# Adaptive-norm columns of the first layer: from GpSimd and VectorE products to TensorE and VectorE, with the opening reordered

## The chip, the cores and the metric

One core of a Trainium2 chip runs the whole program. The metric is device microseconds (us) of one execution. Its engines are TensorE (PE; its weight loads are PEld), VectorE (DVE), ScalarE (ACT), GpSimd (POOL) and SyncE (SP), which here issues most transfers. TensorE's clock is granted at one of two levels, 1.2 and 2.4 GHz; the profile gives the granted share of 2.4 GHz as PEclk.

## What is computed

Two layers over 512 tokens of width 1024. What matters here is how a layer begins:

```python
c_act = jax.nn.silu(c)                                   # (1, 1024)
mod = (c_act @ w_ada[l] + b_ada[l])[:, None, :]          # 6 x 1024
shift1, scale1, gate1, shift2, scale2, gate2 = jnp.split(mod, 6, axis=-1)
h = rms_norm(x, norm1_g[l]) * (1.0 + scale1) + shift1
z = h @ w_in[l]                                          # 14 tiles of 128 columns
```

From z come windowed attention, a short convolution and a multi-scale pooling, one output projection, then a second norm with shift2 and scale2 and an expert layer that takes most of the time.

## The kernel before

x is held transposed, 1024 channels as 8 blocks of 128 partitions by 512 tokens. So shift1 and scale1 are 8 columns each (block c, 128 partitions by 1). Every fp32 operand of a projection is split in two fp32r tiles, a high part rounded to fp32r and a low part, the rest; a product is then three: high by high, high by low, low by high (`mm`, L292 to L294). For h the parts are `hh` and `hl`, for a weight tile (128 output columns of `w_in`, 128x1024) `wh` and `wl`, made by a cast on ScalarE (`prep_hi`, L264) and a subtraction (`prep_lo`, L273, on the engine that is passed).

`setup` (from L108) loads c, makes an identity and three iotas on GpSimd, computes silu of c, and spreads it over all partitions into `cact` (128x1024): eight diagonal tiles on VectorE (L154), eight fp32 products with a tile of 1/1024 on TensorE (L155), two evictions with a factor of 1024 on ScalarE (L156).

`mixer` for the first layer opens so. SyncE's queue gets the four pieces of x (L391), then the first 7 of 16 column tiles of w_ada (each 128 output channels by 1024 inputs, 512 KB, shift and scale of block 0, of block 1, and so on) into buffers that are only needed later, and 4 weight tiles in between. A transfer whose buffer is not free stops what is behind it on the queue. The squares of x go two by two: ScalarE squares (L466), VectorE adds the two (L467), and TensorE sums over channels with fp32 products (`norm_sum`, L349) into `ms`. Each column tile is then multiplied by `cact` and summed along its row. For a scale column VectorE does both in one instruction (L219); for a shift column GpSimd multiplies (L217) and ScalarE sums in `fix` (L452). Then `ada_fix` adds the bias (L226) and, for the scale, multiplies by the norm's gain (L229), all on 128x1. `rsqrt` (from L326) turns `ms` into `rn` by Ln and Exp on ScalarE and a Newton step on VectorE, in halves of 256 tokens. GpSimd makes the low parts of the first three weight tiles before the projection begins.

`norm_apply` is a generator: per block, x times scale times `rn` on VectorE (L367), the shift added on ScalarE, giving `hh` (L368), and `hl` on VectorE (L361), one block behind. `chunk_multi` runs the first three output tiles of the projection together: for each block c it calls `step(c)` (the fix of block c + 2, the next `norm_apply` step, two more columns), then three tiles by three products. After block 5 it prepares one more weight tile in the spare buffer `ch`. The order of the program is the order of each engine; the framework adds the waits. After these 72 products, the other tiles of the projection follow one by one (`chunk`), with the other columns of w_ada worked in by `bg`.

Of the kernel before, what the change touches and what calls it, by code (L numbers as in the profile page):

```python
# [10 lines left out]
F32 = mybir.dt.float32  # L11
# [11 lines left out]
P = 128  # L23
# [58 lines left out]
class Build:  # L82
# [24 lines left out]
    def setup(self):  # L107
        nc, cp, A = self.nc, self.cp, self.A  # L108
        t = lambda shape, dt, nm: cp.tile(shape, dt, name=nm, tag=nm)
        self.x = t([P, NC, S], F32, "x")  # L110
        self.hh = t([P, NC, S], F32R, "hh")
        self.hl = t([P, NC, S], F32R, "hl")
        self.hc = [self.hh[:, c] for c in range(NC)]
        self.lc = [self.hl[:, c] for c in range(NC)]
        self.eps = t([P, 1], F32, "eps")
        nc.vector.memset(self.eps, EPS)
        cc = t([P, NC], F32, "cc")
        nc.sync.dma_start(cc, A["c"])
        self.ident = t([P, P], F32, "ident")
        make_identity(nc, self.ident)  # L120
        self.onesD = t([P, P], F32, "onesD")
        nc.vector.memset(self.onesD, 1.0 / D)
        self.iota = t([P, P], F16, "iota")
        nc.gpsimd.iota(self.iota, pattern=[[1, P]], base=0, channel_multiplier=0,
                       allow_small_or_imprecise_dtypes=True)
        self.iota4 = t([P, P, 4], F16, "iota4")
        nc.gpsimd.iota(self.iota4, pattern=[[1, P], [0, 4]], base=0, channel_multiplier=0,
                       allow_small_or_imprecise_dtypes=True)
        self.iotaA = t([P, TOPK, TOPK], F16, "iotaA")
        nc.gpsimd.iota(self.iotaA, pattern=[[1, TOPK], [0, TOPK]], base=0, channel_multiplier=0,  # L130
                       allow_small_or_imprecise_dtypes=True)
        self.rn = t([P, S], F32, "rn")
        self.modp = {}
        self.ready_parts = set()
        self.par = {}
        for l in range(self.depth):
            for nm in ("b_ada", "norm1", "norm2"):
                w = 48 if nm == "b_ada" else 8
                b = t([P, w], F32, f"{nm}{l}")
                nc.gpsimd.dma_start(b, A[nm][l])  # L140
                self.par[nm, l] = b
# [6 lines left out]
        self.cact = t([P, D], F32, "cact")  # L148
        dg = self.wp.tile([P, NC, P], F32, tag="wr", name="dg", bufs=WR)
        for half in range(2):  # L150
            b = self.bankA()
            for j in range(4):
                c = half * 4 + j
                nc.vector.tensor_scalar(dg[:, c], self.ident, e[:, c:c + 1], None, ALU.mult)  # L154
                nc.tensor.matmul(b[:, j * P:(j + 1) * P], self.onesD, dg[:, c], start=True, stop=True)  # L155
            nc.scalar.activation(self.cact[:, half * 512:(half + 1) * 512], b, AF.Copy, scale=float(D))  # L156

    def setup2(self, tp):
        nc, cp, A = self.nc, self.cp, self.A
# [49 lines left out]
        self.nc.sync.dma_start(w, self.A["w_ada"][l, part * NC + c])  # L209
        return w  # L210

    def ada_col(self, l, part, c, w=None, pool=False):
        nc = self.nc
        if w is None:
            w = self.ada_load(l, part, c)
        if pool:
            nc.gpsimd.tensor_tensor(w, w, self.cact, ALU.mult)  # L217
            return
        nc.vector.scalar_tensor_tensor(w, w, 1.0, self.cact, ALU.mult, ALU.mult,  # L219
                                       accum_out=self.modp[l, part][:, c:c + 1])  # L220

# [80 lines left out]
            self.prep_lo(eng)  # L302
        self.mm(ps, w, hh, hl, width, range(NC), 0, NC - 1)

    def chunk_multi(self, pss, hh, hl, step, eng=None, spare=None):
        n = len(pss)
        while len(self.half) + len(self.ready) < n:
            self.prep_hi()
        while len(self.ready) < n:
            self.prep_lo(eng)  # L310
        ws = [self.ready.pop(0) for _ in range(n)]
        for c in range(NC):
            step(c)
            for ps, w in zip(pss, ws):
                self.mm(ps, w, hh, hl, S, [c], 0, NC - 1)
            if c == (3 if n < 3 else 5):
                hi, lo = spare or (None, None)
                self.prep_hi(hi)
                self.prep_lo(eng, lo)


    def tables(self):
# [54 lines left out]
    def mixer(self, l, ada):  # L377
        nc, tc, A, x = self.nc, self.tc, self.A, self.x
        hh, hl, hc, lc = self.hh, self.hl, self.hc, self.lc
        with tc.tile_pool(name=f"mix{l}", bufs=1) as mp, \  # L380
# [45 lines left out]
            ap1 = self.norm_apply(tmp_, x, l, 1)  # L426
            spare = None
            if l == 0:

                flat = lambda a: a.rearrange("p a b -> p (a b)")  # L430
                prs = [flat(t([P, 4, 384], F32, "pr", bufs=3))[:, 0:D] for _ in range(3)]
                ch_, qk_ = flat(ch), flat(qk)
                slots = [qk_[:, 0:D], qk_[:, D:2 * D], *prs, flat(trig), cst[:, 0:D]]
                slot = lambda k: slots[k if k < 7 else (k - 7) % 6]
                spare = (ch_[:, 0:D], ch_[:, D:2 * D])
                loaded, used = [0], [0]

                def col_load():
                    k = loaded[0]
                    if k < 2 * NC:  # L440
                        loaded[0] += 1
                        self.ada_load(0, k % 2, k // 2, slot(k))

                def col_use():
                    k = used[0]
                    if k < 2 * NC:
                        used[0] += 1
                        self.ada_col(0, k % 2, k // 2, slot(k), k % 2 == 0)

                def fix(c):  # L450
                    w = slot(2 * c)
                    nc.scalar.activation(w, w, AF.Copy, accum_out=self.modp[0, 0][:, c:c + 1])  # L452
                    for part in range(2):
                        self.ada_fix(0, part, c, c + 1)
                    while loaded[0] < 2 * NC and loaded[0] - (7 if loaded[0] < 13 else 6) <= 2 * c + 1:
                        col_load()

                for k in range(7):
                    col_load()
                    if k in (1, 3, 5, 6):  # L460
                        self.prep_raw()
                ms = bankC()
                for c in range(0, NC, 2):
                    sq = [tmp_(), tmp_()]
                    for z in range(2):
                        nc.scalar.activation(sq[z], x[:, c + z], AF.Square)  # L466
                    nc.vector.tensor_tensor(sq[0], sq[0], sq[1], ALU.add)  # L467
                    if c == 0:
                        self.norm_eps(sq[0])
                    self.norm_sum(ms, sq[0], c == 0, c == NC - 2)  # L470
                self.tables()
                for k in range(4):
                    col_use()
                self.prep_hi()
                self.prep_lo(nc.gpsimd)
                for c in range(2):
                    fix(c)
                self.rsqrt(tmp_, ms, P, self.rn)
                for k in range(2):
                    self.prep_hi()  # L480
                    self.prep_lo(nc.gpsimd)
                for k in range(2):
                    col_use()
                next(ap1)
                for k in range(2):
                    col_use()

                def step(c):
                    nonlocal pre
                    if c + 2 < NC:  # L490
                        fix(c + 2)
                    next(ap1, None)
                    for k in range(2):
                        col_use()
                    if c == 5:
                        pre = self.setup2(mp)
                        next(pre)
                        pre = self.stepper(pre)
                        loads()
            else:  # L500
                for k in range(2):
                    self.prep_raw()
                loads()
                step = lambda c: next(ap1, None)
            bg = self.stepper(ada)

# [15 lines left out]
            n0 = 3 if l == 0 else 2  # L522
            pss = [self.bankA(), self.bankA()] + ([bankB()] if l == 0 else [])
            self.chunk_multi(pss, hc, lc, step, nc.gpsimd, spare)
            next(ap1, None)
            for i in range(n0):
                qk_raw(i, pss[i])
            self.prep_hi()
# [756 lines left out]
def layout(inp):  # L1285
# [19 lines left out]
    o["norm1"] = cvec(f("norm1_g"), NC)  # L1305
    o["norm2"] = cvec(f("norm2_g"), NC)
    o["w_ada"] = np.ascontiguousarray(f("w_ada").transpose(0, 2, 1).reshape(L, 48, P, D))
    o["b_ada"] = cvec(f("b_ada"), 48)
    o["w_in"] = chunks(f("w_in")[:, :, cols])
    o["q_norm_g"] = f("q_norm_g")  # L1310
# [33 lines left out]
```

## Time and profile before

| | |
|---|---|
| median of 3 runs | 2924.76 us (2924.71 to 2928.68) |
| profiled execution | 2922.05 us, span 2920.3 us |
| TensorE busy | 2840.1 us, 97% of the span |
| VectorE / ScalarE / GpSimd busy | 82% / 43% / 31% |
| DMA | 782.74 MB, mean 268 GB/s |

The share of busy time is a mean over stages with different limits. The opening is the first 67 us or so, a small part of the span, and has to be read by itself in the timeline and in busy times by stretch. A releaser in brackets is what ended an engine's idle time before an instruction.

### The profile page before, as it was taken

How to read it: one execution, taken by the hardware profiler on the slowest of the kernel's cores; microseconds unless marked ns; L12 is line 12 of the kernel's file. 1: busy time of each engine (PE TensorE's matmuls, PEld its weight loads, DVE VectorE, ACT ScalarE, POOL GpSimd, SP SyncE). 2: the span in 40 equal slices, each digit the busy share in tenths (PEclk: the TensorE clock that was granted, in tenths of full speed). 3: DMA queues.
4: the chain of work that ended last, by engine and by line, in shares of the span. 5: the costliest groups of instructions: out<-in, count | busy, mean ns of one | idle time of the engine just before them, and what ended most of it. 6: DMA issues, size and time to landing. Idle time of an engine off the chain costs nothing.

```text
span 2920.3 us, 41477 instructions
## 1 busy us (share of the span) xinstructions
PE 2840.1 (97%) x15196; PEld 2479.3 (85%) x15196; DVE 2399.2 (82%) x4616; ACT 1267.5 (43%) x1774; POOL 911.5 (31%) x783
## 2 busy tenths in 40 slices
PE   5999999999999999999999999999999999999999
PEld 3667899998888888888866678999988888888887
DVE  7977999858888888888868689999588888887887
ACT  4343357763333333333342444687433333333332
POOL 5415500003334334434324243000133333333332
PEclk8999999999999999999999999999999999999999
DMA  6534257789999999999943323576899999999996
GB/s 231 167 108 125 90 174 257 247 308 324 346 353 370 347 347 361 358 354 358 324 133 132 106 82 118 191 256 249 296 345 337 341 341 332 339 338 345 330 337 223
DMA packets 312972, 782.74 MB, mean 268 GB/s; under 512 B 26784, under 2 KB 154176, under 8 KB 309696
## 3 DMA queue, kind: packets, MB, share of 16 engines
q1 hardware_dynamic: 218992, 438.68, 44.3%
q0 software_dynamic: 73920, 268.53, 25.0%
q10 hardware_dynamic: 19856, 72.88, 6.8%
q8 instruction: 119, 1.95, 0.3%
q14 instruction: 85, 0.70, 0.1%
HBM read 705.02 MB, written 74.97 MB: 267 GB/s over the span
## 4 chain that ended last, share of the span: by engine, by line
PE 81%; DVE 16%; ACT 1%; issue 1%; POOL 0%; DMA 0%; DVEq 0%; ACTq 0%; POOLq 0%
PE pa L292 13%; PE pa L294 13%; PE pa L293 13%; PE pb L1058 6%; PE pb L1059 6%; PE pb L1062 6%; PE pb L1061 6%; PE pb L1057 6%; PE pb L1060 6%; PE pb L1004 1%; PE pb L1005 1%; DVE I L1187 1%; DVE s L1183 1%; DVE I L1181 1%; DVE mx L686 1%
## 5 line engine op out<-in xcount | busy, mean ns | idle before, releaser
L292 PE MATMUL pa<-hh,wh 128*128 128x384 f32 (+1 forms) x2568 | 904.7, 352 | 28.0 <-ACT hh L368 24.4
L293 PE MATMUL pa<-hl,wh 128*128 128x384 f32 (+1 forms) x2568 | 892.3, 347 | 10.9 <-DVE hl L361 10.3
L294 PE MATMUL pa<-hh,wl 128*128 128x384 f32 (+1 forms) x2568 | 892.7, 348 | 2.2 <-DVE wl L273 2.2
L1039 DVE TENSOR_TENSOR vl<-vr,vh 128x1024 fp32r<-128x1024 f32 x256 | 313.6, 1225 | 287.4 <-ACT vh L1038 286.4
L292 PEld LDWEIGHTS pa<-hh,wh 128*128 128x128 f32 x2568 | 484.4, 189 | 70.0 <-ACT hh L368 26.7
L293 PEld LDWEIGHTS pa<-hl,wh 128*128 128x128 f32 x2568 | 484.4, 189 | 40.2 <-DVE hl L361 14.4
L294 PEld LDWEIGHTS pa<-hh,wl 128*128 128x128 f32 x2568 | 483.8, 188 | 23.9 <-DVE wl L273 2.8
L1038 ACT CAST vh<-vr 128x1024 fp32r<-128x1024 f32 x256 | 269.5, 1053 | 507.4 <-PE pb L1062 236.2
L1075 POOL DMA_INDIRECT row<-in_peer_u_dram,eidx x256 | 306.9, 1199 | 550.8 <-DVE acc L1088 408.9
L1084 POOL DMA_INDIRECT row<-in_peer_v_dram,eidx x256 | 307.8, 1202 | 462.9 <-DVE row L1079 412.6
L273 DVE TENSOR_TENSOR wl<-wr,wh 128x1024 fp32r<-128x1024 f32 x264 | 324.0, 1228 | 67.7 <-ACT wh L264 33.7
L264 ACT CAST wh<-wr 128x1024 fp32r<-128x1024 f32 x331 | 349.0, 1056 | 44.2 <-DMA wr<-in_peer_uT_dram 21.5
L1088 DVE SCALAR_TENSOR_TENSOR acc<-row,gw,acc 128x1024 f32<-128x1024 f32 x256 | 327.6, 1280 | 0.1
L1079 DVE SCALAR_TENSOR_TENSOR row<-row,htok 128x1024 f32<-128x1024 f32 x256 | 311.8, 1219 | 0.0
L1058 PE MATMUL pb<-vh,whi 128*128 128x512 f32 x768 | 300.7, 392 | 0.0
L1059 PE MATMUL pb<-vl,whi 128*128 128x512 f32 x768 | 300.5, 391 | 0.0
L1062 PE MATMUL pb<-vh,wlo 128*128 128x512 f32 x768 | 300.0, 391 | 0.0
L1061 PE MATMUL pb<-vh,wlo 128*128 128x512 f32 x768 | 299.3, 390 | 0.0
L1057 PE MATMUL pb<-vh,whi 128*128 128x512 f32 x768 | 298.9, 389 | 0.0
L1060 PE MATMUL pb<-vl,whi 128*128 128x512 f32 x768 | 298.5, 389 | 0.0
L832 ACT ACTIVATE ga<-pa 128x384 f32<-128x384 f32 x256 | 125.8, 491 | 387.5 <-PE pa L294 382.8
L1007 ACT ACTIVATE stg<-pb 128x512 f32<-128x512 f32 x192 | 198.3, 1162 | 33.3 <-PE pb L1005 27.6
(302 smaller groups left out, 3751.7 us busy)
## 6 DMA issues: line engine op xcount, KB each, us to landing
wr<-in_peer_uT_dram SPq DMA_DIRECT2D x256, 512.0 KB
vr<-in_peer_v_dram SPq DMA_DIRECT2D x256, 512.0 KB
Gd<-stg ACTq DMA_DIRECT2D x24, 2048.0 KB
adaw<-in_w_ada_dram SPq DMA_DIRECT2D x80, 512.0 KB
gtFalse<-Gd SPq DMA_DIRECT2D x36, 768.0 KB
Sd<-ga ACTq DMA_DIRECT2D x112, 192.0 KB
gtTrue<-Gd SPq DMA_DIRECT2D x28, 768.0 KB
gs<-Sd SPq DMA_DIRECT2D x112, 192.0 KB
```

Of the source, the lines that this page charges most:

```text
L264: self.nc.scalar.copy(hi, raw)
L273: (eng or self.nc.vector).tensor_tensor(lo, raw, hi.bitcast(F32), ALU.subtract)
L292: nc.tensor.matmul(ps[:, :width], wh, hh[c][:, :width], start=c == first, stop=False)
L293: nc.tensor.matmul(ps[:, :width], wh, hl[c][:, :width], start=False, stop=False)
L294: nc.tensor.matmul(ps[:, :width], wl, hh[c][:, :width], start=False, stop=c == last)
L1057: nc.tensor.matmul(y0, a, vh[:, 0:512], start=f, stop=False)
L1058: nc.tensor.matmul(y1, a, vh[:, 512:1024], start=f, stop=False)
L1059: nc.tensor.matmul(y0, a, vl[:, 0:512], start=False, stop=False)
L1060: nc.tensor.matmul(y1, a, vl[:, 512:1024], start=False, stop=False)
L1061: nc.tensor.matmul(y0, z, vh[:, 0:512], start=False, stop=e)
L1062: nc.tensor.matmul(y1, z, vh[:, 512:1024], start=False, stop=e)
L1088: nc.vector.scalar_tensor_tensor(acc, r, wb[bt - 1][:, k:k + 1], acc, ALU.mult, ALU.add)
```

## The change

It touches the first layer's opening alone.

- The table load of ScalarE comes first; the identity is made after two iotas; an unused constant goes. Silu stays as a 128x8 tile `silu`; `spread` makes `cact` later, with both evictions on VectorE.
- Shift columns: the host lays out a further copy of those rows of w_ada (`w_shift`, inputs on partitions), and TensorE multiplies each of 8 tiles of 128x128 by one column of `silu`, adding in a PSUM bank. VectorE adds the bias. Scale columns stay on VectorE, with the gain folded into two operands (`gb`).
- GpSimd has no products of columns, and the low parts of the weight tiles are made on VectorE.
- Each square is summed by itself on TensorE, eight in place of four pairs. 8 + 6 products into an unused bank stand before and after the spread.
- `chunk_multi` and `norm_apply` are replaced in the first layer by an order written out: `high` (L367 and L368 before), `low` (L361 before), `shift`, `scale`, `weight`, `mul` (three products of tile k and block c).

```diff
+        self.tables()
...
-            nc.scalar.activation(self.cact[:, half * 512:(half + 1) * 512], b, AF.Copy, scale=float(D))
+            nc.vector.tensor_scalar(self.cact[:, half * 512:(half + 1) * 512], b, float(D), None, ALU.mult)
...
-        if pool:
-            nc.gpsimd.tensor_tensor(w, w, self.cact, ALU.mult)
-            return
...
+                        nc.sync.dma_start(slot(k), A["w_ada"][0, NC + k // 2] if k % 2 else A["w_shift"][k // 2])
+
+                def shift(c):
+                    for k in range(NC):
+                        nc.tensor.matmul(col(shp, c), slot(2 * c)[:, k * P:(k + 1) * P], col(self.silu, k),
+                                         start=k == 0, stop=k == NC - 1)
+
+                def scale(c):
+                    w = slot(2 * c + 1)
+                    nc.vector.scalar_tensor_tensor(w, w, 1.0, self.cact, ALU.mult, ALU.mult, accum_out=col(m1, c))
+                    nc.vector.scalar_tensor_tensor(col(m1, c), col(m1, c), col(g_, c), col(gb, c), ALU.mult, ALU.add)
+                    nc.vector.tensor_tensor(col(m0, c), col(shp, c), col(b_ada, c), ALU.add)
                     while loaded[0] < 2 * NC and loaded[0] - (7 if loaded[0] < 13 else 6) <= 2 * c + 1:
                         col_load()
 
+                def high(c):
+                    tmp = tmp_()
+                    nc.vector.scalar_tensor_tensor(tmp, x[:, c], col(m1, c), self.rn, ALU.mult, ALU.mult)
+                    nc.scalar.activation(hh[:, c], tmp, AF.Identity, bias=col(m0, c))
+                    return tmp
+
+                def low(c, tmp):
+                    nc.vector.scalar_tensor_tensor(hl[:, c], tmp, col(m0, c), hh[:, c].bitcast(F32),
+                                                   ALU.add, ALU.subtract)
...
-                    if k in (1, 3, 5, 6):
+                    if k in (1, 3):
                         self.prep_raw()
+                    if k == 3:
+                        self.prep_raw()
+                idle = bankB()
+                self.warm(idle, 8)
                 ms = bankC()
...
+                for c in range(NC):
+                    sq = tmp_()
+                    nc.scalar.activation(sq, x[:, c], AF.Square)
                     if c == 0:
...
+                        self.norm_eps(sq)
+                        self.spread()
+                        self.warm(idle, 6)
+                    self.norm_sum(ms, sq, c == 0, c == NC - 1)
+                nc.vector.scalar_tensor_tensor(gb, b_ada[:, NC:2 * NC], 1.0, g_, ALU.add, ALU.mult)
+                shift(0)
+                scale(0)
                 self.rsqrt(tmp_, ms, P, self.rn)
...
+                mul = lambda k, c: self.mm(pss[k], ws[k], hc, lc, S, [c], 0, NC - 1)
+                tmp = high(0)
+                weight(1)
+                shift(1)
+                scale(1)
+                low(0, tmp)
+                tmp = high(1)
+                mul(0, 0)
+                weight(2)
+                low(1, tmp)
+                mul(0, 1)
+                mul(1, 0)
+                mul(1, 1)
+                shift(2)
+                mul(2, 0)
+                mul(2, 1)
+                scale(2)
+                for c in range(2, NC):
+                    tmp = high(c)
+                    if c + 1 < NC:
+                        shift(c + 1)
+                        scale(c + 1)
+                    low(c, tmp)
+                    for k in range(n0):
+                        mul(k, c)
+                    if c == 4:
+                        self.prep_hi()
+                        self.prep_lo(None, ch_[:, 0:D])
                     if c == 5:
                         pre = self.setup2(mp)
...
+    o["w_shift"] = chunks(f("w_ada")[:, :, 0:D])[0]
```

`weight(k)` calls `prep_hi` k times, then `prep_lo` k times on VectorE.

## Rows read from the trace of the kernel before

**Rows 1.** busy time by stretch: us, engines (instructions), granted clock PEclk, DMA share, GB/s

```profile
20.00:38.00 18.00, 0.00 (x0) 0.00 (x0) 17.93 (x15) 2.56 (x5) 16.14 (x7) 0.50 0.45 183
...
67.00:150.00 83.00, 80.63 (x315) 55.29 (x314) 73.72 (x103) 26.90 (x36) 38.63 (x22) 1.00 0.53 171
```

**Rows 2.** groups of instructions, 20 to 38 us: busy us, mean ns, idle before

```profile
L226 DVE TENSOR_TENSOR mod<-mod,b_ada 128x1 f32<-128x1 f32 x4 | 4.7, 1220 | 0.0
L229 DVE SCALAR_TENSOR_TENSOR mod<-mod,norm 128x1 f32<-128x1 f32 x2 | 4.5, 2228 | 0.1
```

**Rows 3.** timeline, first three projection columns: start us, us, engine, line

```profile
39.75 0.79 PE L292 MATMUL pa<-hh,wh 128*128 128x512 f32 x1 [22.51 <-ACT hh L368]
...
42.67 0.74 DVE L361 SCALAR_TENSOR_TENSOR hl<-tmp,mod,hh 128x512 fp32r<-128x512 f32 x1
...
66.44 0.39 PE L293 MATMUL pb<-hl,wh 128*128 128x512 f32 x1
66.67 0.39 PE L294 MATMUL pb<-hh,wl 128*128 128x512 f32 x1
```

**Rows 4.** timeline, GpSimd: its first products of columns, and the transfers they wait for

```profile
11.40 2.34 POOL L217 TENSOR_TENSOR qk<-qk,cact 128x1024 f32<-128x1024 f32 x1 [4.66 <-DMA qk<-in_w_ada_dram]
...
15.12 2.90 POOL L217 TENSOR_TENSOR pr<-pr,cact 128x1024 f32<-128x1024 f32 x1 [1.38 <-DMA pr<-in_w_ada_dram]
```

**Rows 5.** timeline, opening: diagonal products, epsilon, a square

```profile
3.61 1.81 DVE L154 TENSOR_SCALAR dg<-ident,ce 128x128 f32<-128x128 f32 x8
...
10.16 0.43 DVE L346 TENSOR_SCALAR tmp<-tmp 128x512 f32<-128x512 f32 x1
...
11.22 0.63 ACT L466 ACTIVATE tmp<-x 128x512 f32<-128x512 f32 x1 [0.26 <-DVE tmp L467]
```

**Rows 6.** fp32 products of 512 columns: two passes at high; the sums of squares (min/median/max ns)

```profile
107.06 1.02 PE L595 MATMUL pb<-qk,consts 128*128 128x512 f32 x2
...
L349 PE MATMUL pb<-tmp,onesD x8: 592/1061/1222, 10.6 to 16.7; 128*128 128x512 f32 x8
```

**Rows 7.** timeline, a later rsqrt that nothing disturbs: first and last of VectorE's six

```profile
90.77 0.75 DVE L338 TENSOR_TENSOR tmp<-rqk 32x256 f32<-32x256 f32 x2 [1.16 <-ACT rqk L336]
...
92.12 0.74 DVE L342 SCALAR_TENSOR_TENSOR rqk<-tmp,rqk 32x256 f32<-32x256 f32 x2
```

**Rows 8.** timeline, operations of one block and of one weight tile

```profile
16.40 1.04 ACT L264 CAST wh<-wr 128x1024 fp32r<-128x1024 f32 x1
...
41.55 0.22 DVE L226 TENSOR_TENSOR mod<-mod,b_ada 128x1 f32<-128x1 f32 x2
...
42.78 0.72 ACT L368 ACTIVATE hh<-tmp,mod 128x512 fp32r<-128x512 f32 x1 [1.38 <-DVE tmp L367]
...
L219 DVE SCALAR_TENSOR_TENSOR pr<-pr,cact 128x1024 f32<-128x1024 f32 x3 | 3.7, 1219 | 0.0
```

**Rows 9.** timeline, weight loads (PEld): fp32r, fp32 at low, fp32 at high, bf16

```profile
3.95 3.49 PEld L155 LDWEIGHTS pa<-dg,onesD 128*128 128x128 f32 x16 [3.95 <-DVE dg L154]
...
101.48 0.19 PEld L292 LDWEIGHTS pa<-hh,wh 128*128 128x128 f32 x1 [0.76 <-ACT wh L264]
...
101.59 0.19 PEld L293 LDWEIGHTS pa<-hl,wh 128*128 128x128 f32 x1
...
166.39 0.45 PEld L683 LDWEIGHTS <-identb 128*128 128x128 bf16 x8 [0.55 <-issue]
...
263.98 0.97 PEld L860 LDWEIGHTS pb<-keys,q 128*128 128x128 f32 x8 [0.42 <-ACT q L888]
```

**Rows 10.** TensorE by stretch (PEclk), and two waits in the timeline

```profile
50.00:51.00 1.00, 0.00 (x0) 1.00 1.08 438
...
58.00:59.00 1.00, 1.00 (x4) 0.50 0.19 23
...
51.60 0.50 PE L293 MATMUL pa<-hl,wh 128*128 128x512 f32 x1 [2.76 <-DVE hl L361]
...
56.83 0.52 PE L293 MATMUL pa<-hl,wh 128*128 128x512 f32 x1 [2.87 <-DVE hl L361]
```

More of the change, by code (lines that the diff above doesn't have):

```diff
@@ L128, in setup @@
                        allow_small_or_imprecise_dtypes=True)
+        self.ident = t([P, P], F32, "ident")
+        make_identity(nc, self.ident)
         self.iotaA = t([P, TOPK, TOPK], F16, "iotaA")
@@ L147, in setup, with spread @@
         nc.vector.tensor_tensor(e, e, cc, ALU.mult)
-        self.cact = t([P, D], F32, "cact")
+        self.silu = e
+    def spread(self):
+        nc, e = self.nc, self.silu
+        self.cact = self.cp.tile([P, D], F32, name="cact", tag="cact")
         dg = self.wp.tile([P, NC, P], F32, tag="wr", name="dg", bufs=WR)
@@ L210, in ada_load, with ada_col @@
         return w
-    def ada_col(self, l, part, c, w=None, pool=False):
+    def ada_col(self, l, part, c, w=None):
         nc = self.nc
@@ L303, in chunk, with chunk_multi @@
         self.mm(ps, w, hh, hl, width, range(NC), 0, NC - 1)
-    def chunk_multi(self, pss, hh, hl, step, eng=None, spare=None):
+    def chunk_multi(self, pss, hh, hl, step, eng=None):
         n = len(pss)
@@ L316, in chunk_multi @@
             if c == (3 if n < 3 else 5):
-                hi, lo = spare or (None, None)
-                self.prep_hi(hi)
-                self.prep_lo(eng, lo)
+                self.prep_hi()
+                self.prep_lo(eng)
     def tables(self):
@@ L425, in mixer @@
             pre = lambda k: None
-            ap1 = self.norm_apply(tmp_, x, l, 1)
-            spare = None
             if l == 0:
@@ L434, in mixer @@
                 slot = lambda k: slots[k if k < 7 else (k - 7) % 6]
-                spare = (ch_[:, 0:D], ch_[:, D:2 * D])
-                loaded, used = [0], [0]
+                col = lambda v_, c: v_[:, c:c + 1]
+                m0, m1 = (self.cp.tile([P, NC], F32, name=f"mod0_{k}", tag=f"mod0_{k}") for k in range(2))
+                self.modp[0, 0], self.modp[0, 1] = m0, m1
+                b_ada, g_ = self.par["b_ada", 0], self.par["norm1", 0]
+                gb = t([P, NC], F32, "gb")
+                shp = bankE()
+                loaded = [0]
                 def col_load():
@@ L441, in col_load @@
                         loaded[0] += 1
[L442 to L454, printed above, removed]
+                        nc.sync.dma_start(slot(k), A["w_ada"][0, NC + k // 2] if k % 2 else A["w_shift"][k // 2])
@@ L458, in mixer @@
                 for k in range(7):
                     col_load()
-                    if k in (1, 3, 5, 6):
+                    if k in (1, 3):
                         self.prep_raw()
+                    if k == 3:
+                        self.prep_raw()
+                idle = bankB()
+                self.warm(idle, 8)
                 ms = bankC()
[L463 to L467, printed above, removed]
-                    if c == 0:
-                        self.norm_eps(sq[0])
-                    self.norm_sum(ms, sq[0], c == 0, c == NC - 2)
@@ L471, in mixer @@
[L471 to L477, printed above, removed]
-                self.rsqrt(tmp_, ms, P, self.rn)
[L479 to L494, printed above, removed]
+                for c in range(NC):
+                    sq = tmp_()
+                    nc.scalar.activation(sq, x[:, c], AF.Square)
+                    if c == 0:
+                        self.norm_eps(sq)
+                        self.spread()
+                        self.warm(idle, 6)
+                    self.norm_sum(ms, sq, c == 0, c == NC - 1)
@@ new lines, in mixer, with weight @@
+                nc.vector.scalar_tensor_tensor(gb, b_ada[:, NC:2 * NC], 1.0, g_, ALU.add, ALU.mult)
+                shift(0)
+                scale(0)
+                self.rsqrt(tmp_, ms, P, self.rn)
+                n0 = 3
+                pss = [self.bankA(), self.bankA(), bankB()]
+                ws = []
+                def weight(k):
+                    for _ in range(k):
+                        self.prep_hi()
+                    for _ in range(k):
+                        self.prep_lo()
+                        ws.append(self.ready.pop(0))
@@ L495, in step @@
+                scale(2)
[8 more added lines that the diff above has]
+                    if c == 4:
+                        self.prep_hi()
+                        self.prep_lo(None, ch_[:, 0:D])
                     if c == 5:
@@ L503, in mixer @@
                 loads()
+                ap1 = self.norm_apply(tmp_, x, l, 1)
                 step = lambda c: next(ap1, None)
@@ L520, in qk_ms @@
                 nc.tensor.matmul(msq[:32], self.selA[:, i], sqs[i], start=i == 0, stop=i == 4)
[L522 to L525, printed above, removed]
+            if l > 0:
+                n0 = 2
+                pss = [self.bankA(), self.bankA()]
+                self.chunk_multi(pss, hc, lc, step, nc.gpsimd)
+                next(ap1, None)
             for i in range(n0):
```

4 lines of the change are left out of this document (removed).

## The prediction

> **What bounds the kernel now.** By the table above the tensor engine is busy 97% of the span, so time lost by it is time of the whole. I read the busy times by stretch first [rows 1]: from 20 to 38 us it has no product at all, at a granted clock of 0.50, while VectorE and GpSimd are full; from 67 to 150 us it is busy 80.6 of 83 us. So what the first layer's opening wins or loses up to about 67 us passes on to the end nearly whole, and only that stretch need be worked out. The groups of lines in the same stretch [rows 2] show why VectorE was so long: a sum of 128x1 elements took a mean of 1.22 us and a 128x1 multiply-add 2.23 us, beside GpSimd's products and subtractions; with GpSimd idle, two such sums take 0.22 us together [rows 8]. In the timeline [rows 3] the first projection product starts at 39.75 after 22.5 us of idleness, the low part of the second block of h starts at 42.67 (ends 43.4), and the last of the 72 products of the first three projection columns starts at 66.67. Such products start 0.23 us apart, so the mark to compare with is **66.9 us**. The opening's 24 us after that first product hold only 16.4 us of products (72 by 0.228).
>
> **The change part by part.** "High" is 2.4 GHz, "low" 1.2 GHz.
>
> *The squares.* The first column of w_ada lands by 11.4 and the third, three transfers later, by 15.1 [rows 4], so a transfer takes about 1.25 us and the pieces of x, which are ahead of them, are there by about 10; the first at about 5.6, an estimate from the same spacing. A square is 0.63, the epsilon 0.43, the eight diagonal products 0.23 each, and the two evictions, 0.7 each on VectorE, as two halves of 256 take there [rows 5, 7]. The spread of silu, which now waits for the first square, is therefore complete at about 10.9, and six warming products end at 11.3. Four pairwise sums on VectorE go, and the tensor engine adds eight squares instead of four. One is two passes; two passes of 512 fp32 columns start 0.43 us apart at high and 0.85 at low (the median and the shortest of L349, 1.06 and 0.59, are passes at the two levels) [rows 6]. Eight cost 6.9 at high and 13.7 at low. At high I get 18.3 us, against 17.2 before; two sums at low would add 1.7. I take high, as warming products now begin as soon as the two iotas stand, near 2.2 us.
>
> *The shift products.* Per column eight fp32 products of one output column, so 16 pairs of weight load and product; 8 columns, 128 pairs, all new on the tensor engine. No row has a one-column product. From below: pairs with bf16 weights start 0.056 apart (8 in 0.45). From above: a load of 0.19 that hides nothing and the 0.16 by which a pass outlasts its spacing [rows 6, 9], 0.35. Nearest are rows with the same weights: two fp32r loads that wait for no product start 0.11 apart, and fp32 pairs of 128 columns 0.111 (8 loads in 0.97, the last 0.19) [rows 9]. I take 0.111: **1.8 us a column at high**. At low the 16 pairs of L155 took 0.21 each, 3.4 us.
>
> The Trainium skill (TensorE: Matmul & The Clock Gate, back-to-back issue gap) puts products of 1 to 64 columns at about 60 cycles, or 25 ns where the issue floor binds; by that as an estimate a column would be 0.4 us and the mark about 61. The same page's section on LDWEIGHTS, about 107 ns for 128 columns, agrees with the 0.11 above, and no row here shows a pair below 0.05.
>
> *The first two blocks.* VectorE adds the first shift sum before the rsqrt in its order, and that sum waits for shift 0: 18.3 + 1.8 + 0.2 of completion and handover + 0.2 = 20.3. Ln and Exp are done by then. VectorE's part of rsqrt is 2.1 to 2.2 (90.77 to 92.86) [rows 7]: **rn at 22.5**. Then one chain, all without GpSimd: high part 0.75, hh 0.72, weight cast 1.04 (it now stands behind hh on ScalarE), weight subtraction 1.22 (a VectorE instruction of the same size as a column's product), scale 1 with its two small sums 1.6, low 0.75, high 0.75, hh 0.72, cast 1.04, two subtractions 2.44, low 0.75 [rows 3, 8], with 0.06 at each change of engine: low part 1 is done at **34.6**, before 43.4. That is a gain of 8.8. GpSimd's four products up to 38 and its three subtractions cost nothing any more; the subtractions are now VectorE's, counted here.
>
> *The loop.* The tensor engine has idled, so eight products go at low, 8 x 0.43 = 3.5 (38.1), then shift 2 at low, 3.4 (41.5), then six at high (42.9). From there each block is a closed ring: shift of the next block 1.8, completion and handover 0.23, VectorE's shift sum 0.16, the low part 0.75 (which stands behind that sum in VectorE's order), handover, and eight of nine products 1.8. That is **4.8 us a block**, where VectorE's own work is 3.1, as it was before. Blocks 2 to 6 end at 66.9; block 7 has no shift behind it and needs 2.3: **69.2**. The extra weight subtraction after block 4 (1.22) fits into VectorE's wait for shift 6, 1.7 long.
>
> *Queues.* SyncE issues as many columns, of the same size; from 11.4 us at 1.25 us each, 16 columns and three weight tiles could be there by 35, so slots decide. The last ones are reissued at scale 4, near 50, for use at 62. The fourth weight tile is queued behind them, lands near 55 and is first used at 69. The table load moved to the start lies in the wait for c; identity and iotas on GpSimd's queue swap places and end at about 3, ahead of the square. Nothing for these.
>
> **Sum.** 69.2 - 66.9 = +2.3 us on the profiled execution's 2922.05 us (span 2920.3). The median of the runs is 2924.76, 2.7 above it, so I forecast 2924.8 + 2.3 = **2927 us**. About 0.2%, 5.9 us, is what a measurement of this kernel can tell from no change, so this counts as the same. With pairs of 0.08 the mark is 65.3, with 0.135 72.2: 2923 to 2930 for this case alone.
>
> **Rivals.**
> *The clock falls in the loop (slower).* In each block the nine products are followed by 3.0 us in which only one-column products, one 512-column product and some 0.9 of idleness come. Before, a gap of 2.87 us after nine products brought the granted clock from 1.00 to 0.50 past 57 us, though it had held over an earlier one of 2.76 [rows 10]. Whether the one-column products hold the clock up, no row shows; that they occupy the engine most of that time speaks against a fall. At low a block is 3.4 + 0.23 + 0.16 + 0.75 + 0.06 + 8 x 0.43 = 8.0, so the six products 2.6, five blocks 40 and the last 3.9 after 41.5 give 88: +21, **2946 us**; with every other block low about 2937. It decides if more than one block falls, as each costs 3.2. The Trainium skill (TensorE: Matmul & The Clock Gate, HAM oscillation) tells of a kernel that starts every burst cold because each follows a wait; the fall at 57 us agrees with it.
>
> *The pairs are cheap and the clock holds (faster).* With 0.056 a pair, shifts 0 to 2 are 0.9 each, and if they and the few products before 34.6 keep the clock high, the ring shrinks to 3.9 and the mark to 60.7: -6.2, **2918.5 us**. For it: nothing in the trace shows that a load with a one-column product can't go faster than one that streams 128. Against: loads that wait for nothing still start 0.11 apart. The three runs differ by 4 us, which takes this side to 2914.
>
> *Pairs don't overlap at all.* At 0.35 the mark is 99: +32, 2957. The rows of L860 speak against it.
>
> *The opening is not what the end waits for.* If a later wait takes up the difference, the time stays at 2925. The dense stretch to 150 us [rows 1] speaks against it.
>
> **How the numbers follow.** The forecast has 0.38. The clock rival has 0.30 and the unoverlapped pairs 0.02, slower together 0.32. Cheap pairs have 0.27, of that 0.27 faster, as every other saving that I have not seen (less stretching of VectorE later in the opening among them) falls there too. The later wait has 0.03, so the same is 0.41. The range goes from 2914 to 2946: it takes in the forecast's own bounds, the cheap pairs with the spread of the runs, and the whole clock rival, and leaves out the unoverlapped pairs.
>
> **What would show it.** Right: rn near 22.5, low part 1 near 34.6, 16 loads of a shift in about 1.8 us at high, blocks 4.8 us apart with VectorE waiting for shp each time, the last of the 72 products near 69, and no 128x1 operation above 0.3 us. A granted clock of 0.50 beyond 45 us shows the clock rival; loads under 0.08 apart the cheap pairs. Wrong in its base would be a difference at 67 us that is gone or doubled by 150 us, or the eight sums of squares ending beyond 22 us because the early products go at low.

## The result, and the profile after

The kernel after the change takes **2953.23 us** (median of 4 runs, 2946.66 to 2955.86) against 2924.74 us before (4 runs beside it, 2922.48 to 2928.68): ratio 1.0093 [1.0072, 1.0113], 28.5 us slower. The forecast was 2927, with a range up to 2946; the time is outside it. The profiled execution took 2954.51 us, 32.5 more than that of before. Four executions of 3263 us and more (one of the kernel before, three of experiments below), far off all others of their kernels, are left out of the medians below. From the page of the kernel after the change: the span, busy time of each engine, and the chain that ended last; the last line is the chain of the kernel before.

```profile
span 2952.7 us, 41740 instructions
...
PE 2892.3 (98%) x15346; PEld 2521.2 (85%) x15346; DVE 2382.8 (81%) x4610; ACT 1259.4 (43%) x1755; POOL 889.2 (30%) x771
...
PE 89%; DVE 9%; ACT 1%; issue 1%; POOL 0%; DMA 0%; DVEq 0%; ACTq 0%; SPq 0%; POOLq 0%
...
PE 81%; DVE 16%; ACT 1%; issue 1%; POOL 0%; DMA 0%; DVEq 0%; ACTq 0%; POOLq 0%
```

TensorE's share of the chain went up by 8 points and VectorE's down by 7. That is over 200 us, more than twice the whole opening, so it is not VectorE's relief there: with the same opening and one unused tile put back (`e1_eps_back`, below) the shares are 82% and 15% again. Two losses have to be told apart, one that is over by 83 us and one that grows up to the end. This table (worked out from the starts of the same products in both traces, us; the first row adds the 0.23 to the next product) shows both:

| mark | before | after | difference |
|---|---|---|---|
| last of the 72 products of the first three projection columns ends | 66.9 | 82.5 | +15.6 |
| key products of layer 1, first | 264.0 | 282.7 | +18.7 |
| y0 products of layer 1, first | 651.8 | 674.2 | +22.4 |
| key products of layer 2, last | 1800.2 | 1829.7 | +29.5 |
| y0 products of layer 2, last | 2908.6 | 2941.1 | +32.5 |

**The opening.** The timeline of the kernel after the change, 19 to 45 us (start, duration, engine, line; in brackets the wait before it):

```profile
21.64 0.16 DVE L456 TENSOR_TENSOR mod<-pb,b_ada 128x1 f32<-128x1 f32 x1 [7.29 <-PE pb L449]
...
34.34 0.74 DVE L467 SCALAR_TENSOR_TENSOR hl<-tmp,mod,hh 128x512 fp32r<-128x512 f32 x1
...
35.13 0.79 PE L293 MATMUL pa<-hl,wh 128*128 128x512 f32 x1 [3.20 <-DVE hl L467]
...
38.71 3.41 PE L449 MATMUL pb<-ce,pr 128*128 128x1 f32 x16
...
42.16 0.16 DVE L456 TENSOR_TENSOR mod<-pb,b_ada 128x1 f32<-128x1 f32 x1 [5.68 <-PE pb L449]
```

Up to the second block things went as forecast. The sum of shift 0 ends at 21.8 (forecast 20.3), the low part of block 1 ends at 35.1 (forecast 34.6, before 43.4 by [rows 3]), and the sums of 128x1 elements take 0.16 instead of the 1.22 of [rows 2]. Then VectorE waits for every shift. The views of waits and of TensorE's stretches, both of the kernel after the change (waits: total, times, longest; stretches: length, busy time with instructions, granted clock, DMA share, GB/s):

```profile
DVE mod L456 <- PE pb L449: 24.2, 6, 5.7
...
ACT wh L264 <- DMA wr<-in_w_in_dram: 4.1, 1, 4.1
```

```profile
24.00:40.00 16.00, 8.34 (x23) 0.50 0.33 114
40.00:52.00 12.00, 11.73 (x40) 0.50 0.37 131
52.00:54.00 2.00, 2.00 (x12) 0.64 0.00 0
54.00:56.00 2.00, 1.44 (x10) 1.00 0.40 29
56.00:58.00 2.00, 2.00 (x8) 0.71 0.71 274
58.00:66.00 8.00, 7.73 (x27) 0.50 0.92 308
...
83.00:150.00 67.00, 66.03 (x250) 1.00 0.49 158
```

The granted clock is 0.50 (1.2 GHz) from 24 to 52 us, though TensorE is recorded busy for 11.73 of the 12 us from 40 on. It is at 1.00 (2.4 GHz) for some three microseconds around 55, falls again, does the same around 69, and rises for good only after 80. A shift at low takes 3.4 us, as forecast for low, and a block 5.8 or 7.9 us in turn (shift starts at 44.69, 52.58, 58.42, 66.32, 72.16) instead of 4.8.

**The rest.** The other 17 us of the profiled pair come in code that the change does not touch. Groups of products over the whole span, shapes apart (busy us, mean ns), of the kernel before and then of the kernel after:

```profile
L1058 PE MATMUL pb<-vh,whi 128*128 128x512 f32 x768 | 300.7, 392 | 0.0
...
L294 PE MATMUL pa<-hh,wl 128*128 128x384 f32 x2048 | 687.9, 336 | 2.2 <-DVE wl L273 2.2
L293 PE MATMUL pa<-hl,wh 128*128 128x384 f32 x2048 | 686.7, 335 | 0.0
```

```profile
L1095 PE MATMUL pb<-vh,whi 128*128 128x512 f32 x768 | 298.8, 389 | 0.0
...
L294 PE MATMUL pa<-hh,wl 128*128 128x384 f32 x2048 | 693.8, 339 | 1.7 <-DVE wl L273 1.7
L293 PE MATMUL pa<-hl,wh 128*128 128x384 f32 x2048 | 693.3, 339 | 0.0
```

Every product of 384 columns of h is recorded 3 to 4 ns longer. The records overlap (335 ns each, while the products start 173 ns apart), so their sums are not elapsed time; the spacing of the starts is. Worked out from both traces behind 90 us, with gaps over 400 ns left out:

| products | number | mean spacing before, ns | after, ns | over all, us |
|---|---|---|---|---|
| of hh and hl, 384 columns | 6141 | 175.7 | 177.6 | +12.0 |
| of hh and hl, 512 columns | about 1490 | 232.4 | 237.5 | +7.6 |
| of vh and vl, 512 columns | 4608 | 227.9 | 226.7 | -5.9 |

That is about 14 net, most of the 17. The timelines show it in the spacing of 512-column products of hh and hl: 0.227 us before (six in 1.36 from 232.31), 0.233 after (nine in 2.10 from 250.73), at a clock of 1.00 in both.

What the change did to those products is in the buffers' places in the program as built. The tile `eps` (4 bytes a partition, read by nothing) was allocated after hh and hl. Without it hh and hl stay (offsets 32896 and 49280), and every buffer allocated later moves down by 32 bytes: wr from 76672 to 76640, wh from 97152 to 97120, wl from 113536 to 113504. Before, h and the weights lie at the same offset modulo 64; after, 32 bytes apart.

By their places behind a switch from one kind of product to another, the medians of the spacing tell more. Before, the first six products of h at 384 columns are 171 to 185 ns apart and all later ones 173 to 174; after, they swing between 174 and 180 and never settle. Products of vh and vl behind products of h do the opposite: before, the first nine are 224 to 236 apart and the later ones 227; after, all are 226 to 227. Products of ch and cl, which moved along with the weights, are 225 to 240 apart after the change in the first seven behind products of h, and 226 to 227 from the eighth on, as all of them were before.

### The profile page after: what moved, and what is told of

Read it like the earlier page. It is cut to its first block, busy times and chain, and to the rows that moved or that the text cites. A ratio compares the mean times of both kernels' runs of the same rounds, so it can differ in the third digit from the quotient of the medians.

```text
span 2952.7 us, 41740 instructions
## 1 busy us (share of the span) xinstructions
PE 2892.3 (98%) x15346; PEld 2521.2 (85%) x15346; DVE 2382.8 (81%) x4610; ACT 1259.4 (43%) x1755; POOL 889.2 (30%) x771
## 4 chain that ended last, share of the span: by engine, by line
PE 89%; DVE 9%; ACT 1%; issue 1%; POOL 0%; DMA 0%; DVEq 0%; ACTq 0%; SPq 0%; POOLq 0%
PE pa L292 15%; PE pa L293 15%; PE pa L294 15%; PE pb L1095 6%; PE pb L1098 6%; PE pb L1096 6%; PE pb L1097 6%; PE pb L1094 6%; PE pb L1099 6%; PE pb L1041 1%; PE pb L1042 1%; PE pb L897 1%; DVE wl L273 1%; PE pb L449 1%; DVE mx L723 1%
## 5 line engine op out<-in xcount | busy, mean ns | idle before, releaser
L292 PE MATMUL pa<-hh,wh 128*128 128x384 f32 (+1 forms) x2576 | 919.3, 357 | 7.1 <-ACT hh L367 1.9
L293 PE MATMUL pa<-hl,wh 128*128 128x384 f32 (+1 forms) x2576 | 907.0, 352 | 12.3 <-DVE hl L467 7.8
L294 PE MATMUL pa<-hh,wl 128*128 128x384 f32 (+1 forms) x2568 | 902.7, 352 | 1.7 <-DVE wl L273 1.7
L1112 POOL DMA_INDIRECT row<-in_peer_u_dram,eidx x256 | 315.5, 1232 | 546.3 <-DVE acc L1125 427.9
L264 ACT CAST wh<-wr 128x1024 fp32r<-128x1024 f32 x332 | 350.3, 1057 | 49.7 <-DMA wr<-in_peer_uT_dram 22.4
L273 POOL TENSOR_TENSOR wl<-wr,wh 128x1024 fp32r<-128x1024 f32 x64 | 158.8, 2493 | 208.4 <-ACT wh L264 172.7
```

Of the source, the lines that this page charges most:

```text
L264: self.nc.scalar.copy(hi, raw)
L273: (eng or self.nc.vector).tensor_tensor(lo, raw, hi.bitcast(F32), ALU.subtract)
L292: nc.tensor.matmul(ps[:, :width], wh, hh[c][:, :width], start=c == first, stop=False)
L293: nc.tensor.matmul(ps[:, :width], wh, hl[c][:, :width], start=False, stop=False)
L294: nc.tensor.matmul(ps[:, :width], wl, hh[c][:, :width], start=False, stop=c == last)
```

## The experiments

Two theories stand for the loss after the opening: the *place* of the buffers, and a *clock* that stays lower all through as an after-effect. For the opening: the *clock* of TensorE in the loop, or the *load* of 128 more products whatever the clock. The kernel before, run beside each group of experiments, had medians of 2924.59, 2925.26, 2924.59 and 2924.18 us (15 to 27 runs). A mark or a clock is that of the one profiled execution of each kernel, a time the median of its runs. Runs of the kernel after spread over 9.2 us and of e1 over 12.6, against 6.2 of the kernel before, so in another execution the clock may rise and fall at other places.

**The tile alone.** `e1_eps_back` is the kernel after with the tile put back; `e2_before_no_eps` is the kernel before without it:

```diff
+        self.eps = t([P, 1], F32, "eps")
+        nc.vector.memset(self.eps, EPS)
```

> The changed kernel with the one unused 4-byte tile back, and its memset. Without that tile every buffer made after hl starts 32 bytes earlier, so the weight tiles wh and wl lie at 32 modulo 64 and hh and hl at 0; with it all four are at 0, as before. Theory (the 17 us lost behind the opening are slower products where the two operands lie 32 bytes apart modulo 64): the 512-column products of hh return from 0.233 to 0.227 us apart, and the time falls by 13 to 18 us against the changed kernel, to 2936 to 2941. Rival (the later loss follows from the opening's own lateness, by transfers or the clock): no change, 2950 to 2955.

> The kernel before without that tile and its memset, nothing else. Theory of the operands' places: the opening ends near 67 as before, and the time rises by 13 to 18 us, to 2938 to 2943. Rival (the opening's lateness): no change, 2922 to 2929.

Measured: e1 2939.89 us, ratio 1.0050 [1.0034, 1.0066], so 13.3 below the kernel after; e2 2937.06, ratio 1.0041 [1.0026, 1.0055], so 12.5 above the kernel before and 1 below what was expected. The opening of e1 is as slow as that of the kernel after (clock 0.50 from 28 to 60, the 72 products end at 83.9).

**The same offset elsewhere, and the mirror.** `e3_before_all_32` keeps `eps` and puts another 4-byte tile ahead of hh, so h and the weights all move to 32 modulo 64. `e4_before_mirror` has that tile and no `eps`: h at 32, weights at 0.

```diff
+        pad = t([P, 1], F32, "pad")
+        nc.vector.memset(pad, 0.0)
         self.hh = ...
```

> The kernel before with a 32-byte tile ahead of hh, so that hh, hl, wh and wl all lie at 32 modulo 64. Theory in its relative form (only operands that differ are slow, as the rows of the products from ch suggest): as before, 2921 to 2929, products 0.227 apart. Rival form (a weight tile that does not start at a multiple of 64 is slow): 2938 to 2943.

> The kernel before with the 32-byte tile ahead of hh and without the 4-byte tile behind hl: hh and hl at 32, wh and wl at 0 modulo 64, the mirror of the changed kernel. Relative form: 2938 to 2943, products 0.233 apart. Rival form (weights at a multiple of 64 are fast): 2921 to 2929.

Measured: e3 2923.46 us, 0.9996 [0.9986, 1.0006]; e4 2936.13 us, 1.0041 [1.0027, 1.0056], 2 below what was expected. The same groups of products over the span, in e2, e3 and e4:

```profile
L1056 PE MATMUL pb<-vh,whi 128*128 128x512 f32 x768 | 298.8, 389 | 0.0
...
L291 PE MATMUL pa<-hl,wh 128*128 128x384 f32 x2048 | 692.6, 338 | 0.0
```

```profile
L1060 PE MATMUL pb<-vh,whi 128*128 128x512 f32 x768 | 301.0, 392 | 0.0
...
L295 PE MATMUL pa<-hl,wh 128*128 128x384 f32 x2048 | 686.6, 335 | 0.0
```

```profile
L1058 PE MATMUL pb<-vh,whi 128*128 128x512 f32 x768 | 298.8, 389 | 0.0
...
L293 PE MATMUL pa<-hl,wh 128*128 128x384 f32 x2048 | 692.8, 338 | 0.0
```

It is the distance that counts: with h and weights both at 0 or both at 32 a product of hl takes 335 ns as recorded and the spacing settles at 173; with 0/32 or 32/0 it takes 338 to 339 and the spacing swings between 174 and 180. In e2 and e4 the opening is that of before (the 72 products end at 66.6 and 66.8), so the clock theory for this part falls. The products of vh move the other way by less (392 to 389). Their tiles and those of `whi` share an offset modulo 64 in all of these programs, at 0 before and in e4, at 32 in e2, e3 and after, so the gain does not come from their own place: they lose the uneven start behind products of h wherever those are slow. How the one brings the other about, no run shows. Nor does a run part the weights from the other buffers allocated later, which all moved with them; that products of h are slow at 512 and at 384 columns alike, in different sections of the program, speaks for their own two operands. So the loss of 28.5 us splits into about 12 (e2 and e4: 12.5 and 11.5) for the tile and 15.3 (e1 against the kernel before) for the opening; together 27.

**The clock, with the same loads.** `e5_wide_64` is e1 with each shift product made of 64 equal columns; loads, order and waits stay.

```diff
-nc.tensor.matmul(col(shp, c), slot(2 * c)[...], col(self.silu, k), ...)
+nc.tensor.matmul(shp[:, c * 64:(c + 1) * 64], slot(2 * c)[...],
+                 col(self.silu, k).broadcast_to([P, 64]), ...)
```

> The changed kernel with the unused tile back (as e1_eps_back) and shift products of 64 equal columns in place of one: the same 16 loads a block, each with a product that streams longer but no longer than a load takes. Clock theory (the loop is slow because the clock is granted at 1.2 GHz, and the one-column products do not hold it up): the granted clock stays at 1.00 in more of 40 to 80 us, the last of the 72 products ends near 69 to 72 in place of 82, and the time is 2925 to 2930. Rival (the low clock comes from the waits in the ring, whatever the shift products stream): as e1_eps_back, 2936 to 2944.

Measured: 2931.31 us, 1.0027 [1.0016, 1.0038], 8.6 below e1 and 1 above what was expected; the 72 products end at 72.3 instead of 83.9. First a stretch of e1, then of e5 (columns as above), then e5's shifts and the cast that follows them in its timeline:

```profile
44.00:60.00 16.00, 15.45 (x52) 0.50 0.39 128
```

```profile
44.00:60.00 16.00, 14.09 (x90) 1.00 0.78 268
...
60.00:64.00 4.00, 2.60 (x6) 0.72 0.31 83
```

```profile
48.54 1.89 PE L451 MATMUL pb<-ce,qk 128*128 128x64 f32 x16
...
51.32 0.43 SPq L254 DMA_DIRECT2D wr<-in_w_in_dram  x1
...
53.30 1.90 PE L451 MATMUL pb<-ce,pr 128*128 128x64 f32 x16
...
56.73 1.05 ACT L266 CAST wh<-wr 128x1024 fp32r<-128x1024 f32 x1 [4.03 <-DMA wr<-in_w_in_dram]
```

The same sixteen loads, with more columns to multiply, go at 2.4 GHz from 44 to 60 where one-column products had 1.2, though less of that stretch is recorded busy (14.09 us against 15.45), and the blocks are 4.76 us apart. Load as such does not explain the loss; the clock does. With the ring at its forecast speed a new wait appears: the fourth weight tile is issued only at 51.32, its cast stands on ScalarE ahead of the high part of block 5, and TensorE waits for that near 61, where the clock dips to 0.72.

**Off the ring, and with less work.** `e6_shift_ahead` is e1 with each shift issued up to three blocks ahead; `e8_one_of_eight` is e1 with one of a column's eight products.

```diff
                 shift(1)
+                shift(2)
+                shift(3)
...
                         mul(k, c)
+                    if c + 3 < NC:
+                        shift(c + 3)
```

```diff
                     for k in range(NC):
+                        if k == 0:
-                        nc.tensor.matmul(col(shp, c), ...)
+                            nc.tensor.matmul(col(shp, c), ..., start=True, stop=True)
```

> As e1_eps_back, with the same products in another order: shift 2 and 3 stand behind shift 1, shift 4 ahead of the products of block 1, and shift 5 to 7 behind the products of blocks 2 to 4, so no sum of VectorE waits for a shift that is still behind products. Ring theory (a block's time is the sum of products, the next shift, its sum and the low part): blocks are 3.1 to 3.9 us apart where the clock is high, the last of the 72 products ends at 59 to 63, and the time is 2917 to 2922, below the kernel before. Rival (the one-column products as such cost the time): the 72 products end at 75 or later, 2932 to 2940.

> As e1_eps_back, with one of the eight products of each shift column; the other seven are left out, so the shift is not the reference's. It prices the shift products themselves. Theory (7 of 8 loads gone from the ring: 3.0 us a block at low, 1.6 at high, and the low clock remains or not): the 72 products end at 58 to 64 and the time is 2917 to 2923. Rival (the ring's waits and not the products make the block): they end at 70 or later, 2929 or more.

Measured: e6 2927.36 us, 1.0002 [0.9993, 1.0011], 72 products done at 69.8; e8 2925.47 us, 0.9997 [0.9988, 1.0006], done at 67.4. Both missed the mark and the time that were expected, by 2 to 7 us. The clock fell in each (e6: 0.50 from 28 to 40 and from 60 to 64), and in e8 the blocks go at 3.2 us (low products of h start at 43.59, 46.73, 49.89) until the same late tile stops them; its timeline:

```profile
56.91 0.80 PE L294 MATMUL pa<-hh,wh 128*128 128x512 f32 x1 [4.77 <-ACT hh L466]
...
59.30 0.63 PE L294 MATMUL pa<-hh,wh 128*128 128x512 f32 x1
```

The 0.63 of the product that waits for nothing is a product at low (0.39 to 0.40 at high, before the wait): a wait of 4.77 us has again cost the clock as well.

**The late tile.** `e10_wide_tile_early` is e5 with the fourth weight tile among the first loads; `e11_ahead_wide_early` has that, the 64 columns and the order of e6.

```diff
-                    if k == 3:
+                    if k in (3, 6):
                         self.prep_raw()
```

> As e5_wide_64 (unused tile back, shift products of 64 columns), with the fourth weight tile issued with the first ones and not in block 4. In e5 hh of block 5 stood on ScalarE behind the cast of that tile, which waited for its transfer, and the blocks before it were 4.76 us apart at the high clock. Theory (ring at the high clock, and that wait): the 72 products end at 69 to 70, as forecast from the rows of before, and the time is 2926 to 2929. Rival (the wait at block 5 has another cause): they end at 72 to 73 as in e5, 2930 to 2933.

> As e6_shift_ahead, with products of 64 columns and the fourth weight tile issued early. Theory (ring opened, clock held, no wait for the tile): the 72 products end at 59 to 62 and the time is 2917 to 2921, below the kernel before by 0.1 to 0.3%. Rival (the clock falls in spite of the wider products, as TensorE waits for VectorE): 64 to 68, 2922 to 2927.

Measured: e10 2928.68 us (2923.26 to 2931.64), 1.0015 [1.0006, 1.0024], the mark at 66.3 (expected 69 to 70); e11 2920.77 us, 0.9986 [0.9977, 0.9995], the mark at 62.1. In e10 the wait near 61 is gone and the blocks stay 4.76 us apart to the end; the profiled execution, 2923.26, is the fastest of its ten, which is why its mark looks better than its median. In e11 blocks are still 4.76 us apart, though the shifts go ahead. VectorE's shift sums in its timeline:

```profile
44.73 0.16 DVE L458 TENSOR_TENSOR mod<-pb,b_ada 128x1 f32<-128x1 f32 x1 [3.15 <-PE pb L451]
49.49 0.16 DVE L458 TENSOR_TENSOR mod<-pb,b_ada 128x1 f32<-128x1 f32 x1 [1.88 <-PE pb L451]
```

The sums of shifts that were done blocks ago wait 3.15 and 1.88 us: all shift columns lie in one PSUM tile, and the sum waits for the latest product that was issued into it, not for its own column.

**What else the opening can give.** `e12_tiles_before_norm` is e11 with two weight tiles prepared ahead of the rsqrt; `e13_sum_after_low` is e12 with the next block's shift sum behind this block's low part on VectorE; `e14_sum_after_low_one_col` is e13 with one-column products again.

```diff
+                scale(0)
+                weight(2)
+                summed(0)
+                self.rsqrt(tmp_, ms, P, self.rn)
```

```diff
                     low(c, tmp)
+                    if c + 1 < NC:
+                        summed(c + 1)
```

> As e11_ahead_wide_early, with two weight tiles cast and subtracted while the sums of squares run, where ScalarE and VectorE idle, and the third after scale 1. Theory (casts and subtractions behind rn were 5.9 us of the chain): low part 1 is done near 31 in place of 35, the 72 products end 3 to 5 us before those of e11, the time is 2912 to 2918. Rival (VectorE's 3.1 us a block from rn on is the bound, not the tiles): as e11.

> As e12_tiles_before_norm, with VectorE's shift sum of the next block behind the low part of this one. In e11 and e12 the blocks were still 4.76 us apart: the sum of shift c+1 waited for the last shift issued ahead of it, as all of them lie in one PSUM bank, and the low part stood behind that sum. Theory (with the order swapped the ring is open, TensorE's 3.9 us a block is the bound): blocks 3.9 us apart, the 72 products end at 55 to 57 in place of 59.5, the time is 2912 to 2918. Rival (hh, which needs the sum, takes the place of the low part in the ring): as e12.

> As e13, with shift products of one column again. Theory (the clock): the granted clock falls below 1.00 between 40 and 60 us as in e6, and the 72 products end 2 to 8 us later than in e13, at 2915 to 2925. Rival (with no wait left in the ring the clock holds with one column as well): as e13.

Measured: e12 2919.41 us, 0.9978 [0.9969, 0.9988], mark 59.4, both short of what was expected; e13 **2917.08 us**, 0.9972 [0.9963, 0.9981], mark 54.5; e14 2921.65 us, 0.9991 [0.9981, 1.0000], mark 62.5. First two of e13's shifts and its clock, then e14's clock:

```profile
41.45 1.89 PE L451 MATMUL pb<-ce,trig 128*128 128x64 f32 x16
...
45.32 1.89 PE L451 MATMUL pb<-ce,qk 128*128 128x64 f32 x16
```

```profile
28.00:40.00 12.00, 11.85 (x61) 0.86 0.67 239
...
44.00:60.00 16.00, 15.45 (x73) 1.00 0.52 184
```

```profile
28.00:40.00 12.00, 10.57 (x41) 0.50 0.37 119
...
44.00:60.00 16.00, 15.54 (x91) 1.00 0.62 202
```

e13 has 3.87 us a block and beats both kernels, by 7 us against the kernel before. e14 differs from it by the columns alone: a clock of 0.50 between 28 and 40 in place of a mean of 0.86, the mark 8 us later, the time 4.6 us. But from 44 on its clock is 1.00 with one-column products too. So these products do not bring the clock down whatever surrounds them: in e14, where a block is 3.87 us, it held once it had risen; in the 5.8 to 7.9 us blocks of the kernel after it did not rise for more than some three microseconds.

In e12 and e13 the time fell by less than the mark (5.2 for 7.5 and 7.1 for 12.4 us by medians, though 9.1 for 12.4 between the profiled executions of e13 and of the kernel before). Where the rest went is not settled.

## Why the prediction was wrong, step by step

*What passes on.* Right. The stretch behind the opening is as dense as in [rows 1] (66.03 of 67 us), and e1, e5, e6, e8, e11 turn a mark that moved by +17.0, +5.4, +2.9, +0.5, -4.8 us into a time that moved by +15.3, +6.1, +2.1, +0.2, -3.8. In e10, e12 and e13 mark and median agree less well, by 2 to 5 us.

*The first two blocks, and GpSimd off VectorE's back.* Right within 1.5 us at each mark: the sums of squares end at 19.8 (forecast 18.3), rn stands at 23.8 (22.5), low part 1 at 35.1 (34.6). The gain of 8 us there is real.

*The price of a pair.* Right: the sixteen pairs of shift 0 take 1.84 us, 0.115 each, against the 0.111 taken from [rows 9], and 3.41 at low against 3.4. The 0.4 us a shift that I estimated from the Trainium skill (TensorE: Matmul & The Clock Gate, back-to-back issue gap) is not borne out. The figure there is for products by themselves; the same section says that in a stream of loads and products both set the spacing, and the trace agrees: sixteen pairs with 64 columns take 1.89 us (e5), hardly more than with one.

*The ring of 4.8 us.* Right as a ring (4.76 in e5 and e10), **wrong in its clock**. The step that failed is "then six at high (42.9). From there each block is a closed ring: shift of the next block 1.8". TensorE did not come back to 2.4 GHz after shift 2. Against the forecast the six products and shift 3 cost 2.5 us more, four rings 8.3 (27.5 instead of 19.2 between the low parts of blocks 2 and 6), the last products 1.9, and 0.6 was lost before: 13.3, which is 82.5 - 69.2. This is the clock rival, to which I gave 0.30; its two versions, every block and every other block low, lie on either side of the blocks seen. The argument against it, that one-column products occupy the engine, was the mistake: 11.73 of 12 us recorded busy went with a clock of 0.50, so busy time in the profile does not tell whether the clock holds.

*The removed tile.* The change drops `eps`, and my sum has no term for it, nor has any rival: about 12 of the 28.5 us. It put the time outside a range that held the whole clock rival (2946); with the tile back (e1, 2939.9) the time is inside. [Rows 1 to 10] could not show it, but the diff could: it changes the places of the operands of every product, and I asked of each line only what it executes.

*The fourth weight tile.* "lands near 55 and is first used at 69" is wrong where the ring runs at its forecast speed: the tile is needed for the cast on ScalarE, which is queued ahead of the high part of block 5, not only for its products. In the kernel after this wait (4.1 us) is hidden by the slow ring; in e5 and e8 ScalarE waits 4.0 and 5.0 us for the tile with the high part of block 5 behind it, and e10 takes that away.

*Slips that changed nothing.* Between the first projection product and the mark lie 27 us (39.75 to 66.9), not 24. The first piece of x would land at 6.4 by the spacing of 1.25; the 5.6 does not follow from it, though the first square did start at 5.36. And with 0.4 us a shift my own ring would have been 3.4 us and the mark near 58, not 61.

## What to carry to other kernels

Before costing a removed or added tile at nothing, look at where the allocator puts what comes after it: in this kernel it paid 12 us to keep the operand and the weights of the hot products at the same offset modulo 64 bytes, and a small pad tells in a few executions whether that matters. Where a stage feeds TensorE many narrow products in a closed ring, take the granted clock as an unknown with a price of its own and measure it with wider products of the same loads. When a ring gets faster, ask again which transfers had been in time only because it was slow.

## What the runs showed of the hardware

Two things that I had not expected. In the two kernels in which h and its weights lie 32 bytes apart modulo 64 and the opening is that of before (e2, e4), products of h are recorded at 338 to 339 ns instead of 335 at 384 columns; their starts, which settle at 173 ns apart otherwise, swing between 174 and 180, and at 512 columns they are 0.234 us apart instead of 0.227. Over this kernel that is 11 to 13 us of 2925, whichever of the two lies at 32. Why the chip does this is open. And in the stretch from 44 to 60 us sixteen weight loads with 64 columns each went at 2.4 GHz where the same sixteen with one column each went at 1.2, which made the wider product the cheaper one: 1.89 us against 3.41.
